# Entry of a Strassen MLP: eight channel pairs instead of four start on the first token half, the second half's sums move from POOL to DVE, and the squared ReLU moves from DVE to ACT

## The chip, the cores and the metric

The kernel runs on one core of one Trainium2 chip. The metric is the device time of one execution in microseconds (us). Engines: PE is TensorE, DVE is VectorE, ACT is ScalarE, POOL is GpSimd, SP is the engine whose queue issues most of the DMA transfers.

## The reference, cut to what matters

The program is a whole two-block network (a gated recurrent mixer with a mixture of experts, then attention with an MLP). The change lies in its last part, the MLP of the second block: 1024 tokens, 1024 features, 4096 hidden channels, a squared ReLU, all in float32.

```python
h = rms_norm_2(x, norm_mlp[i]) * (1 + sc_f) + sh_f
x = x + g_f * (jnp.square(jax.nn.relu(h @ w_mlp_in[i])) @ w_mlp_out[i])
```

## The kernel before, in words

**Split numbers.** Each float32 operand of a matmul is split into a high and a low part: `Net.split` (L65 to L67) lets ACT write the high part (L66) and DVE the difference (L67). A product of two 128-row tiles is three matmuls (L854 to L856).

**Seven products.** `h @ w_mlp_in` is done by Strassen's scheme in Winograd's form. The tokens are two halves of 512, the features two halves of 512, and the hidden channels 16 *pairs* of 2 x 128. For each pair n there are seven products, numbered by o; one *step* is one product of one pair, 12 matmuls of 128x512 into one PSUM tile (`X`, or `Z` for o = 3). The whole is 112 steps. The moving operands are the seven tiles `hc[0]` to `hc[6]`. `hc[0]` and `hc[1]` are the first token half as it is; `hc[2]` to `hc[6]` are sums in which the second half takes part. So products 0 and 1 of a pair need only the first half, and the other five need the second half. The weights (`wc`) of products 0, 1, 4 and 6 are raw blocks; those of 3, 2 and 5 are sums that POOL makes in `Mlp.prep` (L1648 to L1656).

**Order.** `Mlp.order` lists the steps: first products 0 and 1 of pairs 0 to 3 (steps 0 to 7), then product 3 of pairs 0 and 1 (steps 8 and 9), products 2, 4, 5, 6 of the same, and so on two pairs at a time. PE keeps this order. `Mlp.todo` lists the weight loads in the same order; a pair that is begun early has its first block loaded twice. The raw blocks pass through a ring of six tiles (`wr`), in which the eight normed token tiles also stand at first. `prep` runs three steps ahead (`LOOK`), with four `wc` buffers.

**The second half.** Ahead of steps 2 to 5, `half1(kk)` (L2350 to L2370) turns one quarter of the features of the second half: 8 transposes on PE into PSUM (`hTp`, two buffers), two evacuations on ACT (L2357), then the sums: two subtractions on DVE (L2360, L2361) make `T`, three on POOL (L2363, L2364, L2368) and one on DVE (L2369) make the others, and five splits write `hc[3]`, `hc[5]`, `hc[2]`, `hc[4]`, `hc[6]`. `T` and POOL's weight sum S1 share the two buffers `hTt`. The temporaries lie in `x2a`, whose tokens were written to DRAM before (`x2d`) and are loaded back later.

**After a product.** For o = 0 ACT copies PSUM to a tile `s`; for the others DVE adds to it. A finished sum passes `Mlp.inner` (L1707): one DVE instruction does max(s,0)*s, and SP stores the result (L1708) to DRAM. After step 111, `Mlp.block` multiplies by `w_mlp_out`; its operands come back through the same ring and are split into the places of `hc` (`item`).

DVE, ACT, POOL and SP keep the order that the scheduler gave them; an instruction that waits holds up all that stand behind it on its engine.

Of the kernel before, what the change touches and what calls it, by code (L numbers as in the profile page):

```python
# [19 lines left out]
P = 128  # L20
# [1555 lines left out]
class Mlp:  # L1576
# [54 lines left out]
    def prep(self, g):  # L1631
# [4 lines left out]
        first = n < 4 and o < 2  # L1636
# [23 lines left out]
        wc = self.wc[g] = self.early.pop(0) if self.early else self.wp.tile([P, 2, 4, P], F32R, name="wc", bufs=4)  # L1660
# [9 lines left out]
    def step(self, g):  # L1670
# [3 lines left out]
        self.prep(g + self.LOOK)  # L1674
# [7 lines left out]
        if o == 0:  # L1682
            s = self.s[n] = self.wp.tile([P, 512], F32, name="s", bufs=4)
            nc.scalar.activation(s, pt, AF.Copy)
        elif o == 1:
            s = self.wp.tile([P, 512], F32, name="c", bufs=4)
            v.tensor_add(s, self.s[n], pt)
            self.inner(s, n, 0, 0)
        elif o == 2:
            v.tensor_add(self.s[n], self.s[n], pt)  # L1690
        elif o == 4:
            s = self.s[n]
            u = self.u[n] = self.wp.tile([P, 512], F32, name="c", bufs=4)
            r = self.wp.tile([P, 512], F32, name="c", bufs=4)
            v.tensor_add(u, s, pt)
            z = self.Z.pop(n)
            v.tensor_add(r, u, z)
            v.tensor_add(s, s, z)
            self.inner(r, n, 1, 1)
        elif o > 4:  # L1700
            s = (self.s if o == 5 else self.u).pop(n)
            v.tensor_add(s, s, pt)
            self.inner(s, n, *((0, 1) if o == 5 else (1, 0)))

    def inner(self, s, n, i, m):

        self.net.nc.vector.scalar_tensor_tensor(s, s, 0.0, s, op0=ALU.max, op1=ALU.mult)  # L1707
        self.net.nc.sync.dma_start(self.rD[n][i][:, HALF[m]], s)  # L1708


    def open_second(self, x2, gate_row, out):
        self.x2, self.out = x2, out
        self.gb = self.wp.tile([P, D], F32, name="mgb", tag="wc", bufs=4)
# [18 lines left out]
    def block(self, c):  # L1732
        net = self.net
        nc, v = net.nc, net.nc.vector
        for tt in range(TT):
# [9 lines left out]
            for n in range(2):  # L1745
                cc = HALF[n]
                t = self.wp.tile([P, 512], F32, name="s", bufs=4)
                v.tensor_mul(t, pts[n], self.gb[:, cc])  # L1748
                v.tensor_add(self.x2[tt][:, cc], self.x2[tt][:, cc], t)
# [21 lines left out]
def program(net, ctx, I, out, dbg):  # L1771
# [21 lines left out]
    x2d = scratch("x2d", [512, D])  # L1793
# [460 lines left out]
    with ExitStack() as cx:  # L2254
# [9 lines left out]
        def units(tts):  # L2264
            for tt, n in tts:
# [6 lines left out]
                    if n == 1 and tt < 4:  # L2272
# [39 lines left out]
        x2 += [xb.tile([P, D], F32, name=f"x2_{tt}") for tt in range(4, 8)]  # L2312
# [7 lines left out]
        mlp.early = []  # L2320

# [28 lines left out]
        def half1(kk):  # L2350

            t12, t22 = tmp[:, kk, :], tmp[:, 4 + kk, :]
            for k, t in ((kk, t12), (kk + 4, t22)):
                pt = nps.tile([P, 512], F32, name="hTp", bufs=2)
                for i, xn in enumerate(xns):
                    nc.tensor.transpose(pt[:, i * P:(i + 1) * P], xn[:, k * P:(k + 1) * P], net.ident)
                nc.scalar.activation(t, pt, AF.Identity, scale=sc3[:, k:k + 1], bias=sh3[:, k:k + 1])  # L2357
            T = np_.tile([P, 512], F32, name="hTt", bufs=2)
            h = [hc[o][:, kk] for o in range(7)]
            v.tensor_sub(T, t12, h[0][:, 0, :].bitcast(F32))  # L2360
            v.tensor_sub(T, T, h[0][:, 1, :].bitcast(F32))  # L2361
            net.split(h[3][:, 0, :], h[3][:, 1, :], T)
            nc.gpsimd.tensor_sub(t12, t22, t12)  # L2363
            nc.gpsimd.tensor_sub(T, t22, T)  # L2364
            net.split(h[5][:, 0, :], h[5][:, 1, :], t22)
            net.split(h[2][:, 0, :], h[2][:, 1, :], T)
            net.split(h[4][:, 0, :], h[4][:, 1, :], t12)
            nc.gpsimd.tensor_sub(t22, h[1][:, 0, :].bitcast(F32), T)  # L2368
            v.tensor_add(t22, t22, h[1][:, 1, :].bitcast(F32))  # L2369
            net.split(h[6][:, 0, :], h[6][:, 1, :], t22)  # L2370

        with tc.manual_schedule(engines={mybir.EngineType.PE}):
            for g in range(len(mlp.order)):
                if g in range(2, 6):
                    half1(g - 2)
# [7 lines left out]
                if g == 20:  # L2383
# [4 lines left out]
                if g >= len(mlp.order) - 6:  # L2388
                    mlp.item()
            for _ in range(2):  # L2390
# [23 lines left out]
```

## Time and profile before

| | |
|---|---|
| median of 3 runs | 2606.24 us (2605.98 to 2619.54) |
| the profiled execution | 2609.64 us, of which the span of the profile is 2607.9 us |
| PE busy | 2386.0 us, 91% of the span |
| DVE, ACT, POOL busy | 77%, 52%, 21% of the span |
| the MLP's steps | from 1911.7 us to 2250.8 us of the span |
| the MLP's second matmul | from 2250.8 us to the end |

Times inside the span count from its start. Busy shares are means over stages with different limits. For a change in one stage what counts is what PE waits for in that stage, since PE is fully busy from 1971 us to the end.

### The profile page before, as it was taken

What the parts mean: (1) busy time and instruction counts of PE and PEld (TensorE: products, weight loads), DVE (VectorE), ACT (ScalarE), POOL (GpSimd) and SP (SyncE); (2) the same over time, 40 slices, a digit from 0 to 9 for tenths busy, and PEclk for the clock granted to TensorE, in tenths of its full rate; (3) what the DMA queues carried; (4) which work ended last, traced back from release to release, by engine and by line L of the source; (5) the groups of instructions that cost most, each with busy time, mean ns of one, the idle gap of its engine ahead of it and who ended that gap; (6) DMA issues with size and microseconds to landing.
All of it is one profiled execution on the core that took longest, in us unless ns stands there. A gap on an engine that the chain in (4) does not pass through costs nothing. (4 is left out here: it accounts for less than half of the span.)

```text
span 2607.9 us, 34881 instructions
## 1 busy us (share of the span) xinstructions
PE 2386.0 (91%) x11789; PEld 1920.5 (74%) x11789; DVE 2014.5 (77%) x3648; ACT 1346.6 (52%) x2447; POOL 551.4 (21%) x527
## 2 busy tenths in 40 slices
PE   6899989959999999985899999997979999999999
PEld 5576767747776766543898999986757888888887
DVE  6888886877989788996787777877668667776664
ACT  5555563236868677775677777775332222321210
POOL 1202121042224243532000000013335233000000
PEclk9899999969999999997999999998989999999999
DMA  7445565769999999994022122017334333532211
GB/s 263 135 138 164 177 203 165 258 231 304 366 340 377 329 362 320 365 366 143 18 50 50 50 49 50 23 39 204 138 89 129 97 113 121 186 103 91 98 65 65
DMA packets 258866, 445.64 MB, mean 171 GB/s; under 512 B 22096, under 2 KB 101828, under 8 KB 258684
## 3 DMA queue, kind: packets, MB, share of 16 engines
q1 hardware_dynamic: 250532, 424.45, 48.8%
q0 software_dynamic: 8032, 18.89, 3.2%
q8 instruction: 94, 1.54, 0.3%
q14 instruction: 88, 0.72, 0.1%
q10 hardware_dynamic: 120, 0.03, 0.0%
HBM read 395.62 MB, written 54.73 MB: 173 GB/s over the span
## 5 line engine op out<-in xcount | busy, mean ns | idle before, releaser
L67 DVE TENSOR_TENSOR wl<-wr,wh 128x1024 fp32r<-128x1024 f32 x210 | 249.9, 1230 | 28.3 <-ACT wh L66 25.7
L66 ACT ACTIVATE wh<-wr 128x1024 fp32r<-128x1024 f32 x216 | 220.6, 1054 | 87.4 <-PE po L464 30.6
L67 DVE TENSOR_TENSOR wl<-x,wh 128x1024 fp32r<-128x1024 f32 x164 | 192.6, 1219 | 26.8 <-ACT wh L66 25.4
L591 POOL DMA_INDIRECT x1d<-y,gidx x56 | 156.5, 2795 | 235.1 <-DMA x1d<-y,gidx 107.3
L66 ACT ACTIVATE hc<-wr 128x1024 fp32r<-128x1024 f32 x64 | 64.6, 1056 | 266.8 <-PE X L855 244.8
L856 PE MATMUL X<-hc 128*128 128x512 f32 x512 | 200.3, 391 | 0.0
L854 PE MATMUL X<-hc 128*128 128x512 f32 x512 | 200.3, 391 | 0.0
L855 PE MATMUL X<-hc 128*128 128x512 f32 x512 | 199.7, 390 | 0.0
L66 ACT ACTIVATE wh<-x 128x1024 fp32r<-128x1024 f32 x168 | 172.8, 1058 | 43.0 <-issue 9.1
L854 PE MATMUL pj<-xh,h2h 128*128 128x384 f32 (+1 forms) x512 | 190.2, 372 | 0.8 <-DVE V L1433 0.7
L1748 DVE TENSOR_TENSOR s<-X,mgb 128x512 f32<-128x512 f32 x128 | 86.5, 690 | 123.2 <-PE X L856 123.1
L855 PE MATMUL pj<-xh,h2l 128*128 128x384 f32 (+1 forms) x512 | 175.9, 344 | 0.0
L856 PE MATMUL pj<-xl,h2h 128*128 128x384 f32 (+1 forms) x512 | 174.6, 342 | 0.0
L854 PE MATMUL X<-hc,wc 128*128 128x512 f32 x384 | 151.9, 396 | 3.4 <-ACT rs_y L91 3.4
L855 PE MATMUL X<-hc,wc 128*128 128x512 f32 x384 | 151.7, 395 | 0.2 <-DVE wc L67 0.2
L856 PE MATMUL X<-hc,wc 128*128 128x512 f32 x384 | 151.4, 394 | 0.0
L782 DVE SCALAR_TENSOR_TENSOR aacc<-aw,cs,aacc 128x512 f32<-128x512 f32 x160 | 128.2, 803 | 25.0 <-DMA aw<-in_w_ada 12.5
L66 ACT ACTIVATE wc<-wr 128x512 fp32r<-128x512 f32 x96 | 60.5, 633 | 166.6 <-PE X L856 118.7
L1501 ACT ACTIVATE Sx<-Sx,mx 128x128 f32<-128x128 f32 (+7 forms) x128 | 99.0, 773 | 41.0 <-DVE mx L1496 40.5
L67 DVE TENSOR_TENSOR pl<-pT,ph 128x512 fp32r<-128x512 f32 (+1 forms) x160 | 100.8, 634 | 23.0 <-ACT ph L66 19.6
L855 PEld LDWEIGHTS X<-hc 128*128 128x128 f32 x512 | 96.1, 188 | 21.2
L856 PEld LDWEIGHTS X<-hc 128*128 128x128 f32 x512 | 96.1, 188 | 21.1
(562 smaller groups left out, 6871.0 us busy)
## 6 DMA issues: line engine op xcount, KB each, us to landing
wr<-in_w_expert_down SPq DMA_DIRECT2D x43, 1024.0 KB
wr<-in_w_expert_up SPq DMA_DIRECT2D x33, 1024.0 KB
x<-in_w_expert_gate SPq DMA_DIRECT2D x32, 1024.0 KB
wr<-in_w_expert_gate SPq DMA_DIRECT2D x32, 1024.0 KB
x<-in_w_expert_up SPq DMA_DIRECT2D x31, 1024.0 KB
aw<-in_w_ada SPq DMA_DIRECT2D x48, 512.0 KB
x<-in_w_expert_down SPq DMA_DIRECT2D x21, 1024.0 KB
aw<-in_ada_w SPq DMA_DIRECT2D x40, 512.0 KB
```

Source lines behind the costliest of these rows:

```text
L66: self.nc.scalar.activation(hi, src, AF.Copy)
L67: (v or self.nc.vector).tensor_sub(lo, src, hi.bitcast(F32))
L591: nc.gpsimd.indirect_dma_start(out=m.xd, out_offset=bass.IndirectOffsetOnAxis(ap=gi[0:r], axis=0), in_=y[o:o + r], in_offset=None, bounds_ ...
L782: nc.vector.scalar_tensor_tensor(acc, t[:, r, :], ccol[:, q:q + 1], acc, op0=ALU.mult, op1=ALU.add)
L854: nc.tensor.matmul(pt, sh, mh, start=first, stop=False)
L855: nc.tensor.matmul(pt, sl, mh, start=False, stop=False)
L856: nc.tensor.matmul(pt, sh, ml, start=False, stop=last)
L1501: nc.scalar.activation(Sx[:, 0:wd], Sx[:, 0:wd], AF.Exp, bias=mx[:, m - 1:m], scale=-1.0, accum_out=sm[:, q:q + 1])
L1748: v.tensor_mul(t, pts[n], self.gb[:, cc])
```

## The change

1. Products 0 and 1 of eight pairs come first, not of four: steps 0 to 15, so that the first step that needs the second half is step 16, not step 8. Four more blocks of 512 KB are loaded. `LOOK` is 4, with five `wc` buffers; at step 4 nothing is prepared and at step 5 two steps' weights.
2. `half1` is cut up. `turn(k)` keeps the transposes and the evacuation ahead of steps 2 to 5. The sums and splits are a generator of 12 parts, one after each step from step 2 to step 13. All six sums are on DVE, none on POOL.
3. `inner` is two ACT instructions (Relu, Square) in place of one on DVE.
4. The sums `s` of products 0 stand in the tile of the other four token tiles (`x2b`), which are therefore written to `x2d` as well and loaded back after the steps.

```diff
-    LOOK = 3
+    LOOK = 4
+    EARLY = 8
...
-        self.order = [(0, 0), (0, 1), (1, 0), (1, 1), (2, 0), (2, 1), (3, 0), (3, 1)]
-        self.todo = [("p", n) for n in range(4)]
+        self.order = [(n, o) for n in range(self.EARLY) for o in range(2)]
+        self.todo = [("p", n) for n in range(self.EARLY)]
...
-            self.order += duo(a, (3, 2, 4, 5, 6) if a < 4 else (0, 1, 3, 2, 4, 5, 6))
+            self.order += duo(a, (3, 2, 4, 5, 6) if a < self.EARLY else (0, 1, 3, 2, 4, 5, 6))
...
-        self.prep(g + self.LOOK)
+        for i in (8, 9) if g == 5 else () if g == 4 else (g + self.LOOK,):
+            self.prep(i)
...
-            s = self.s[n] = self.wp.tile([P, 512], F32, name="s", bufs=4)
+            s = self.s[n] = self.sums[:, n % 8, :]
...
-        self.net.nc.vector.scalar_tensor_tensor(s, s, 0.0, s, op0=ALU.max, op1=ALU.mult)
+        self.net.nc.scalar.activation(s, s, AF.Relu)
+        self.net.nc.scalar.activation(s, s, AF.Square)
         self.net.nc.sync.dma_start(self.rD[n][i][:, HALF[m]], s)
...
-                    if n == 1 and tt < 4:
+                    if n == 1:
                         nc.sync.dma_start(x2d[tt * P:(tt + 1) * P, :], x2[tt])
...
-            nc.gpsimd.tensor_sub(t12, t22, t12)
-            nc.gpsimd.tensor_sub(T, t22, T)
...
-            nc.gpsimd.tensor_sub(t22, h[1][:, 0, :].bitcast(F32), T)
-            v.tensor_add(t22, t22, h[1][:, 1, :].bitcast(F32))
...
+        def half1():
+
+            for kk in range(4):
+                t12, t22 = tmp[:, kk, :], tmp[:, 4 + kk, :]
+                T = np_.tile([P, 512], F32, name="hTt", bufs=2)
+                h = [hc[o][:, kk] for o in range(7)]
+                v.tensor_sub(T, t12, h[0][:, 0, :].bitcast(F32))
+                v.tensor_sub(T, T, h[0][:, 1, :].bitcast(F32))
+                net.split(h[3][:, 0, :], h[3][:, 1, :], T)
+                yield
+                v.tensor_sub(T, t22, T)
+                net.split(h[2][:, 0, :], h[2][:, 1, :], T)
+                v.tensor_sub(t12, t22, t12)
+                net.split(h[4][:, 0, :], h[4][:, 1, :], t12)
+                yield
+                net.split(h[5][:, 0, :], h[5][:, 1, :], t22)
+                v.tensor_sub(T, h[1][:, 0, :].bitcast(F32), T)
+                v.tensor_add(T, T, h[1][:, 1, :].bitcast(F32))
+                net.split(h[6][:, 0, :], h[6][:, 1, :], T)
+                yield
...
                 mlp.step(g)
-                if g == 20:
+                if g > 1:
+                    next(parts, None)
+                if g == 40:
```

Three places show how the built programs differ. The first is POOL from its first instruction in the MLP. Before, with the four quarters' sums (`x2a`, `hTt_20194` to `hTt_20337`) and the weight sums of pair 0 (`wr_20354`, `wr_20358`) in one queue:

```order
L2363 TENSOR_TENSOR x2a_18854<-x2a_18854 128x512
L1648 TENSOR_TENSOR hTt_20370<-wr_20354 128x512
L1650 TENSOR_TENSOR wr_20354<-wr_20358,wr_20354 128x512
L1651 TENSOR_TENSOR wr_20358<-hTt_20370,wr_20358 128x512
L1656 TENSOR_TENSOR wr_20358<-wr_20358 128x512
L2364 TENSOR_TENSOR hTt_20337<-x2a_18854,hTt_20337 128x512
L2368 TENSOR_TENSOR x2a_18854<-hc1_19613,hTt_20337 128x512
```

Now only the weight sums of pairs 0 and 1 stand there:

```order
L1649 TENSOR_TENSOR hTt_20504<-wr_20311 128x512
L1651 TENSOR_TENSOR wr_20311<-wr_20325,wr_20311 128x512
L1652 TENSOR_TENSOR wr_20325<-hTt_20504,wr_20325 128x512
L1657 TENSOR_TENSOR wr_20325<-wr_20325 128x512
L1649 TENSOR_TENSOR hTt_20529<-wr_20313 128x512
```

The last quarter's two sums no longer stand behind pair 0's weights; twelve POOL instructions are gone, and nothing in the MLP's entry waits for POOL but the weights of products 3, 2 and 5.

The second place is ACT around the last two pairs of transposes before (`hTp_20278`, `hTp_20284` are the third quarter's):

```order
L2357 ACTIVATE x2a_18854<-hTp_20235,cols2_4810,sc3_4815 128x512
L66 ACTIVATE hc2_20132<-hTt_20194 128x512
L66 ACTIVATE hc5_20135<-x2a_18854 128x512
L66 ACTIVATE hc3_20133<-hTt_20241 128x512
L66 ACTIVATE hc4_20134<-x2a_18854 128x512
L66 ACTIVATE hc6_20136<-x2a_18854 128x512
L66 ACTIVATE wc_20258<-wr_20145 128x512
L2357 ACTIVATE x2a_18854<-hTp_20278,cols2_4810,sc3_4815 128x512
```

and now, from the second to the third quarter (`hTp_20226`, `hTp_20259`):

```order
L2360 ACTIVATE x2a_18854<-hTp_20226,cols2_4810,sc3_4815 128x512
L66 ACTIVATE wc_20232<-wr_20133 128x512
L66 ACTIVATE hc2_20138<-hTt_20215 128x512
L66 ACTIVATE hc4_20140<-x2a_18854 128x512
L66 ACTIVATE wc_20319<-wr_20303 128x512
L2360 ACTIVATE x2a_18854<-hTp_20259,cols2_4810,sc3_4815 128x512
L1709 ACTIVATE c_20248<-c_20248 128x512
L2360 ACTIVATE x2a_18854<-hTp_20265,cols2_4810,sc3_4815 128x512
L1710 ACTIVATE c_20248<-c_20248 128x512
```

Between two evacuations there stood five splits of the sums; now there stand two, and Relu and Square (L1709, L1710) between others.

The third place is DVE ahead of the weights of step 17, the second step that needs the second half (`wc_20531`, made from POOL's sum `hTt_20529`); `hTt_20499` is the last quarter's `T`:

```order
L67 TENSOR_TENSOR wc_20506<-hTt_20504,wc_20506 128x512
L2372 TENSOR_TENSOR hTt_20499<-x2a_18854,hTt_20499 128x512
L2374 TENSOR_TENSOR x2a_18854<-x2a_18854 128x512
L67 TENSOR_TENSOR hc5_20141<-x2a_18854,hc5_20141 128x512
L67 TENSOR_TENSOR hc2_20138<-hTt_20499,hc2_20138 128x512
L67 TENSOR_TENSOR hc4_20140<-x2a_18854,hc4_20140 128x512
L67 TENSOR_TENSOR wc_20531<-hTt_20529,wc_20531 128x512
L1689 TENSOR_TENSOR c_20547<-x2b_19608,X_20534 128x512
```

Before, these stood ahead of the weights of the same product (`wc_20394`):

```order
L67 TENSOR_TENSOR hc3_20133<-hTt_20337,hc3_20133 128x512
L67 TENSOR_TENSOR wc_20372<-hTt_20370,wc_20372 128x512
L1687 TENSOR_TENSOR c_20388<-s_20323,X_20375 128x512
L67 TENSOR_TENSOR hc2_20132<-hTt_20337,hc2_20132 128x512
L2369 TENSOR_TENSOR x2a_18854<-x2a_18854,hc1_19613 128x512
L1707 SCALAR_TENSOR_TENSOR c_20388<-c_20388 128x512
L67 TENSOR_TENSOR wc_20394<-hTt_20392,wc_20394 128x512
```

The last operand `hc3` that both steps read is now done before pair 0's weights, with five of the last quarter's operations between the two weights. The loads of ACT's tables are three in either program.

## Rows read from the trace of the kernel before

**Rows 1.** Windows: stretch, length, busy (count) PE, PEld, DVE, ACT, POOL; clock; DMA.

```profile
1911.00:1930.20 19.20, 18.31 (x84) 14.84 (x84) 14.51 (x22) 10.76 (x21) 5.77 (x4) 0.91 0.34 96
1930.20:1971.00 40.80, 22.76 (x70) 16.67 (x69) 36.56 (x38) 16.01 (x28) 26.93 (x17) 0.71 0.44 126
2040.00:2240.00 200.00, 200.00 (x877) 164.21 (x876) 140.68 (x195) 59.01 (x91) 64.50 (x40) 1.00 0.40 126
2240.00:2602.00 362.00, 362.00 (x1584) 296.84 (x1582) 233.41 (x325) 56.16 (x58) 0.00 (x0) 1.00 0.28 95
```

**Rows 2.** Waits of PE, 1905 to 2608 us: total us, times, longest.

```profile
PE Z L854 <- ACT wc L66: 7.3, 1, 7.3
PE Z L855 <- DVE wc L67: 6.8, 2, 4.1
PE hTp L2356 <- ACT x2a L2357: 4.0, 2, 3.3
```

**Rows 3.** Timeline of PE: start, duration, and what ended the idle time before.

```profile
1911.69 0.47 PE L854 MATMUL X<-hc,wc 128*128 128x512 f32 x1 [3.38 <-ACT rs_y L91]
...
1919.37 1.03 PE L2356 MATMUL hTp<-ident,wr 128*128 128x128 f32 x8
1920.16 0.48 PE L854 MATMUL X<-hc,wc 128*128 128x512 f32 x1
...
1959.33 0.63 PE L856 MATMUL Z<-hc,wc 128*128 128x512 f32 x1
...
1963.60 0.54 PE L854 MATMUL Z<-hc,wc 128*128 128x512 f32 x1
1966.84 0.56 PE L855 MATMUL Z<-hc,wc 128*128 128x512 f32 x1 [2.70 <-DVE wc L67]
```

**Rows 4.** Chain that ended last, in order of time: start, duration, what.

```profile
1956.55 1.59 POOL wr L1656
1958.14 1.70 POOL hTt L2364
...
1965.04 1.76 DVE wc L67
```

**Rows 5.** Groups of instructions, 1911 to 1971 us: count, busy us, mean ns, idle before.

```profile
L2357 ACT ACTIVATE x2a<-hTp,cols,sc 128x512 f32<-128x512 f32 x8 | 5.8, 771 | 0.0
L2356 PE MATMUL hTp<-ident,wr 128*128 128x128 f32 x32 | 5.3, 313 | 4.0 <-ACT x2a L2357 4.0
```

**Rows 6.** Timeline of DVE, POOL and SP's queue at four places.

```profile
1917.93 0.69 DVE L67 TENSOR_TENSOR wc<-wr,wc 128x512 fp32r<-128x512 f32 x1 [2.61 <-ACT wc L66]
...
1944.95 0.69 DVE L67 TENSOR_TENSOR hc<-hTt,hc 128x512 fp32r<-128x512 f32 x1
1945.55 0.69 DVE L2360 TENSOR_TENSOR hTt<-x2a,hc 128x512 f32<-128x512 f32 x1
1945.71 1.65 POOL L2364 TENSOR_TENSOR hTt<-x2a,hTt 128x512 f32<-128x512 f32 x1 [2.07 <-DVE hc L67]
1946.15 1.76 DVE L67 TENSOR_TENSOR hc<-x2a,hc 128x512 fp32r<-128x512 f32 x1
...
1975.44 0.38 SPq L1620 DMA_DIRECT2D wr<-in_w_mlp_in  x1
1979.70 1.29 POOL L1648 TENSOR_TENSOR hTt<-wr 128x512 f32<-128x512 f32 x1 [11.78 <-DMA wr<-in_w_mlp_in]
```

**Rows 7.** Groups of instructions, 1975 to 2240 us.

```profile
L66 ACT ACTIVATE wc<-wr 128x512 fp32r<-128x512 f32 x81 | 51.5, 635 | 157.3 <-PE X L856 114.9 <-PE Z L856 26.0 <-issue 10.1
L1707 DVE SCALAR_TENSOR_TENSOR c<-c 128x512 f32<-128x512 f32 x40 | 27.2, 681 | 0.0
L66 ACT ACTIVATE hc<-wr 128x1024 fp32r<-128x1024 f32 x9 | 9.5, 1060 | 7.0 <-DMA wr<-rD 3.9 <-DMA wr<-in_w_mlp_out 2.4 <-PE X L856 0.7
```

**Rows 8.** Groups of instructions, 1850 to 1971 us: Square with a sum.

```profile
L820 ACT ACTIVATE wr<-x 128x1024 f32<-128x1024 f32 x4 | 4.2, 1060 | 23.1 <-DVE x L2270 23.1
```

**Rows 9.** Timeline of PE: the first matmul of `Mlp.block`.

```profile
2250.80 0.39 PE L854 MATMUL X<-hc 128*128 128x512 f32 x1
```

More of the change, by code (lines that the diff above doesn't have):

```diff
@@ L1635, in prep @@
         gp = self.net.nc.gpsimd
-        first = n < 4 and o < 2
+        first = n < self.EARLY and o < 2
         f = self.raw["p" if first else "f", n]
@@ L1659, in prep @@
             src = A22
[L1660 removed]
+        wc = self.wc[g] = self.early.pop(0) if self.early else self.wp.tile([P, 2, 4, P], F32R, name="wc", bufs=5)
         self.net.split(wc[:, 0], wc[:, 1], src)
@@ L1692, in step @@
             s = self.s[n]
-            u = self.u[n] = self.wp.tile([P, 512], F32, name="c", bufs=4)
-            r = self.wp.tile([P, 512], F32, name="c", bufs=4)
+            u = self.u[n] = self.wp.tile([P, 512], F32, name="c", bufs=5)
+            r = self.wp.tile([P, 512], F32, name="c", bufs=5)
             v.tensor_add(u, s, pt)
@@ L1712, in open_second @@
         self.x2, self.out = x2, out
-        self.gb = self.wp.tile([P, D], F32, name="mgb", tag="wc", bufs=4)
+        self.gb = self.wp.tile([P, D], F32, name="mgb", tag="wc", bufs=5)
         self.net.nc.sync.dma_start(self.gb, gate_row.to_broadcast([P, D]))
@@ L1746, in block @@
                 cc = HALF[n]
-                t = self.wp.tile([P, 512], F32, name="s", bufs=4)
+                t = self.wp.tile([P, 512], F32, name="c", bufs=5)
                 v.tensor_mul(t, pts[n], self.gb[:, cc])
@@ L1792, in program @@
     x1d = scratch("x1d", [S, D])
-    x2d = scratch("x2d", [512, D])
+    x2d = scratch("x2d", [S, D])
     rD = [[scratch(f"rD{n}_{i}", [P, S]) for i in range(2)] for n in range(Mlp.NP)]
@@ L2311, in program @@
         xb = net.pool(cx, "x2b")
-        x2 += [xb.tile([P, D], F32, name=f"x2_{tt}") for tt in range(4, 8)]
+        x2b = xb.tile([P, 4, D], F32, name="x2b")
+        x2 += [x2b[:, tt, :] for tt in range(4)]
         hc = {o: xb.tile([P, 4, 2, 512], F32R, name=f"hc{o}") for o in range(2)}
@@ L2320, in program @@
         mlp.early = []
+        mlp.sums = x2b.rearrange("p t (a n) -> p (t a) n", a=2)
         def norm(tt, t):
@@ L2348, in program @@
         tmp = x2a.rearrange("p t (a n) -> p (t a) n", a=2)
[L2350 to L2362, printed above, removed]
-            nc.gpsimd.tensor_sub(t12, t22, t12)
-            nc.gpsimd.tensor_sub(T, t22, T)
-            net.split(h[5][:, 0, :], h[5][:, 1, :], t22)
-            net.split(h[2][:, 0, :], h[2][:, 1, :], T)
-            net.split(h[4][:, 0, :], h[4][:, 1, :], t12)
-            nc.gpsimd.tensor_sub(t22, h[1][:, 0, :].bitcast(F32), T)
-            v.tensor_add(t22, t22, h[1][:, 1, :].bitcast(F32))
-            net.split(h[6][:, 0, :], h[6][:, 1, :], t22)
@@ new lines, in turn @@
+        def turn(k):
+            pt = nps.tile([P, 512], F32, name="hTp", bufs=2)
+            for i, xn in enumerate(xns):
+                nc.tensor.transpose(pt[:, i * P:(i + 1) * P], xn[:, k * P:(k + 1) * P], net.ident)
+            nc.scalar.activation(tmp[:, k, :], pt, AF.Identity, scale=sc3[:, k:k + 1], bias=sh3[:, k:k + 1])
+        def half1():
[17 more added lines that the diff above has]
+                yield
@@ L2372, in program @@
+        parts = half1()
         with tc.manual_schedule(engines={mybir.EngineType.PE}):
@@ L2374, in program @@
                 if g in range(2, 6):
-                    half1(g - 2)
+                    for k in (g - 2, g + 2):
+                        turn(k)
                     if g == 5:
@@ L2389, in program @@
                     mlp.item()
+            for tt in range(4, 8):
+                nc.sync.dma_start(x2[tt], x2d[tt * P:(tt + 1) * P, :])
             for _ in range(2):
```

2 lines of the change are left out of this document (1 added, 1 removed).

## The prediction

> **What bounds the kernel now.** I read the windows by stage first. From 2040 to 2240 us and from 2240 us to the end PE is busy throughout at full clock, so nothing there but fewer matmuls could make the end come sooner; 877 matmuls in 200.00 us are 0.228 us each, and a step of 12 is 2.74 us [rows 1]. The stretch before is another thing: from 1930.20 to 1971.00 us PE is busy 22.76 of 40.80 us, with a mean granted clock of 0.71 [rows 1]. Whatever PE loses there the end pays in full, because PE is never idle behind it.
>
> The list of PE's waits says for what: 7.3 us until ACT had the high part of the first weights of product 3, 6.8 us until DVE had low parts of such weights (two waits), 4.0 us until ACT had emptied a PSUM buffer of the transposes [rows 2]. PE's timeline shows that the waits drag a second loss behind them. Behind the second of them, ten matmuls from 1959.33 to 1963.60 us are 0.43 us apart: that is the lower of the two clock levels, 1.2 GHz and not 2.4, and it lasts for some us after PE is at work again [rows 3].
>
> The chain that ended last shows who was late. It goes through POOL: a weight sum (L1656), then the last quarter's second sum (L2364), and from there over ACT and DVE to the low part at 1965.04 us [rows 4]. POOL's sums are also slow, and slow for DVE: beside a POOL sum of 1.65 us, a DVE subtraction with both inputs in SBUF took 1.76 us; the two ahead of it took 0.69 us and began 0.60 us apart [rows 6].
>
> **How much there is to win.** In the 40.80 us stand 70 instructions: eight transposes (the last of the four groups that make the 32 [rows 5]) and 62 matmuls. At full rate these are 62 x 0.228 = 14.1 us and 1.0 us (a group of eight took 1.03 us [rows 3]), together 15.1 us. So 40.80 - 15.1 = 25.7 us are lost: 18.1 us of waits and 7.6 us of low clock and overlap. In the stretch ahead of it 84 instructions (60 matmuls, 24 transposes) should take 13.7 + 2.4 us, and take 18.5 us from the first matmul at 1911.69 us on [rows 3]; these 2.4 us, low clock after the idle time ahead of the MLP, I leave in place, since the change does nothing ahead of step 0.
>
> **Part by part.**
>
> *Steps 8 to 15 moved ahead.* No matmul is added. Step 16 is the first to need the second half. With PE at full rate it comes 14 steps (2 to 15) and four groups of transposes after 1919.37 us; a group takes 0.79 us of PE's time, from 1919.37 to 1920.16 us [rows 3]. That is 1919.4 + 38.4 + 3.2 = 1961.0 us, and step 17 follows at 1963.7 us. Before, the same product of the same pair had its last late weights at 1966.8 us [rows 3]. So if the work on the second half were done no sooner than before, PE would still wait 3 us; what it has lost is the chain through POOL, and what it has gained is DVE work. Whether that is done by 1964 us is worked out below.
>
> *Transposes.* Before, five splits of late sums stood on ACT between two evacuations; now two do, and Relu and Square come in between. None of them waits for POOL. An evacuation takes 0.77 us [rows 5]; PE comes for the buffer a step of 2.74 us later. I cost these waits at 0 (before 4.0 us, plus their low clock). If an evacuation came behind four other ACT instructions of 0.63 us and a wait for DVE, PE would wait a us or so; that is within the range.
>
> *Sums to DVE.* From the low part at 1917.93 us [rows 6] to that of step 17's weights DVE has 61 instructions, as the program lists them. At 0.60 us apart that is 36.6 us, until 1954.5 us. POOL now runs eight weight sums of about 1.65 us shortly before step 16, 13 us of contention. In the third place above, six DVE instructions with both inputs in SBUF stand in that time, each 1.76 - 0.69 = 1.07 us longer: 6.4 us, so 1960.9 us. What is not in this sum is how long DVE waits for ACT's high parts. In the stretch before it was busy 36.56 of 40.80 us [rows 1]; waits of 10% here too, some 4 us, would bring 1965 us against a need at 1964 us. The wait of PE at step 17 thus lies between 0 (no waits, 1961 us) and 7 us (eight slowed instructions in POOL's 13 us and not six, 2 us, and twice the waits, 8 us: 1971 us). I take 1 us, the sum with the share of waits that the rows show.
>
> *Squares to ACT.* No row shows a Relu by itself; I price both by the copy of 128x512, 0.63 us, and by Square on twice the width, 1.06 us [rows 7, 8], so 1.26 us on ACT in place of 0.68 us on DVE. Up to the weights of step 17 ACT has 60 instructions from about 1917 us on, just ahead of DVE's low part at 1917.93 us: 8 x 0.77 + 52 x 0.63 = 38.9 us even without overlap, so 1956 us, earlier than DVE. In the steady steps ACT's idle time ahead of its weight splits alone is 157.3 us of 265 us [rows 7]; of the 64 squares 56 fall behind step 15, and 56 x 1.26 = 71 us fit into it. I cost them at 0; the cover is ACT's idle time and the four steps by which `prep` runs ahead. The Trainium skill speaks against this edit: the page "ScalarE: Activation LUTs", section "Rules for kernel authors", wants relu and mul on VectorE, not on ScalarE. By the rows, the rule is right on busy time (1.26 us against 0.68 us), and the sum is the same with it or without, as long as neither engine is the one that PE waits for; what it would do if ACT were that engine is rival D.
>
> *Loads and stores.* Four more blocks of weights, four more token tiles out and back: 12 transfers of 512 KB on SP's queue. A weight load landed 4.3 us after its issue (1975.44 to 1979.70 us [rows 6]). Step 8, the first with a block of the new four, is due at 1919.4 + 3.2 + 6 x 2.74 = 1939.0 us, and the ring's last slots come free with step 5's transposes at about 1931 us. Of these 8 us a load and its split (4.3 + 0.63 + 0.69 us) leave 2 us, so they are covered. The reloads go into buffers that become free pair by pair. The DMA engines were busy 40% of the time in the steps [rows 1]. Cost 0; what it costs without cover is rival C.
>
> **The sum.** -25.7 us for the stretch, +1 us at step 17, 0 for the rest: -24.7 us. The profiled execution took 2609.64 us, which gives 2585. It was 3.4 us above the median of the runs, so against the median of 2606.24 us I forecast 2582 us.
>
> **Rivals.** Measurement of this kernel can tell about 0.5%, 13 us, from no change.
>
> *A, the forecast* (0.60): 2582 us, own range 2578 to 2587.
>
> *B, DVE becomes the bound of the entry* (0.27). PE waits 5 us at step 17, between my value and the upper end, then runs some ten matmuls at 0.43 us, 2 us more, and waits once more about 2 us at step 18 or 19, whose weights stand behind on DVE. 2606.2 - 25.7 + 9 = 2589.5 us. For it: 61 instructions and 13 us of contention in 44 us leave no slack in my sum. Against it: the sum ends on the needed time, not 5 us behind.
>
> *C, the win is given back at the start of `block`* (0.08). Its operands come through SP's queue behind the stores, which now wait for Square on ACT, and their splits (1.06 us) stand on ACT between Relu and Square. Before, nine of them were done by 2240 us [rows 7] and `block` began at 2250.80 us [rows 9]: 10.8 us of cover. If each of the eight that the first block needs came 3 us later, PE would wait 24 - 11 = 13 us: 2606.2 - 24.7 + 13 = 2595 us, and with low clock and a second wait 2600 us. It decides from 1.4 us a split on. Against it: `prep` and loads run further ahead than before.
>
> *D, slower: ACT is too slow in the steady steps* (0.05). A Relu waits for a DVE sum, and the weight splits behind it on ACT wait too. If PE then lost 0.7 us in each of the 96 steps from 16 on, 67 us, the time would be 2606.2 - 24.7 + 67 = 2649 us; it is slower than before from 0.26 us a step. Against it: ACT's 157.3 us of idle time [rows 7]. The rule of the Trainium skill's page "ScalarE: Activation LUTs" would speak for it.
>
> That the change does not do what it says is excluded by the listing of the built program: POOL's twelve sums are gone and 16 steps stand ahead of the first `Z`.
>
> **Range and chances.** 2576 takes in the forecast with the 2.4 us of low clock gone as well; 2594 takes in B with some us more. Outside lie C, D and tails, about 0.17. Faster by over 0.5%: A, B and half of C, 0.90; same 0.06; slower 0.04.
>
> **What the profile will show.** Right, if PE's waits from 1911 us on come to 1 to 2 us instead of 18.1 us, the first `Z` starts at about 1961 us, the clock stays 1.00 from 1916 us on, `block` begins at about 2226 us, and POOL's first instruction in the entry is a weight sum. B would show as a wait of `Z` L855 for DVE's `wc` with DVE fully busy ahead of it and instructions of 1.7 us in it. C shows as waits of `X` for `hc` at 2226 us, D as many short waits of `X` for ACT's `wc`. Wrong altogether, if PE has as many matmuls at 0.43 us as before.

## The result, and the profile after

| | before | after |
|---|---|---|
| median of the runs | 2606.63 us (4 runs, 2605.98 to 2619.54) | 2581.76 us (4 runs, 2577.85 to 2583.37) |
| ratio after to before | | 0.9892, 95% interval 0.9865 to 0.9920 |
| profiled execution, its span | 2609.64, 2607.9 us | 2582.41, 2580.4 us |
| first matmul of step 0 | 1911.69 us | 1910.34 us |
| first matmul of `block` [rows 9] | 2250.80 us | 2223.21 us |
| the 112 steps between these two | 339.11 us | 312.87 us |
| from the first matmul of `block` to the end of the span | 357.1 us | 357.2 us |

Faster by 24.9 us, about 1.1%. The change lies in the 112 steps, and so does the gain: they became 26.2 us shorter. The stretch behind them is as long as before. The 1.35 us ahead of step 0 belong to a part that the change hardly touches; it varies from execution to execution by much more (last section). So from here on each kernel is judged by its runs and by **the length of the 112 steps in its profile**, which leaves that part out. Medians and ratios leave out one execution that lies far off all others (2740.64 us, of the kernel with the squares back on DVE).

Windows of after, in the columns of [rows 1]:

```profile
1911.00:1930.20 19.20, 19.18 (x93) 15.90 (x94) 15.89 (x29) 14.63 (x27) 0.00 (x0) 0.91 0.48 137
1930.20:1971.00 40.80, 40.80 (x178) 33.09 (x177) 37.15 (x50) 26.65 (x48) 12.83 (x8) 1.00 0.63 189
2012.41:2212.41 200.00, 200.00 (x878) 164.54 (x877) 118.06 (x154) 108.12 (x170) 56.03 (x40) 1.00 0.43 139
2040.00:2240.00 200.00, 200.00 (x877) 164.34 (x876) 119.06 (x157) 105.61 (x165) 44.27 (x32) 1.00 0.48 157
```

The second row is the whole result. In the same 40.80 us in which PE did 70 instructions before, it now does 178, at full clock. The third row shows the price of the steady steps; it is the 200 us that lie as far ahead of `block` as the window from 2040 to 2240 us did before. ACT went from 59.01 to 108.12 us of work, DVE from 140.68 to 118.06, the DMA share from 0.40 to 0.43, and PE's count is the same to one, 878 matmuls. (In the last row, the old window, 17 us belong to `block`; PE's count is 877 there.)

All waits of PE from 1890 us to the end, where [rows 2] had 18.1 us in three kinds:

```profile
PE X L854 <- ACT rs_y L91: 3.4, 1, 3.4
PE X L855 <- DVE wc L67: 0.2, 1, 0.2
```

Both stand ahead of and in step 0; the first was there before ([rows 3], at 1911.69 us). Behind step 0 PE never waits. Its timeline at four places: step 0, the first group of transposes, steps 16 and 17 (the first products 3), and the first matmul of `block`:

```profile
1910.34 0.47 PE L854 MATMUL X<-hc,wc 128*128 128x512 f32 x1 [3.38 <-ACT rs_y L91]
...
1918.03 1.04 PE L2359 MATMUL hTp<-ident,wr 128*128 128x128 f32 x8
...
1960.69 0.40 PE L854 MATMUL Z<-hc,wc 128*128 128x512 f32 x1
...
1963.41 0.39 PE L854 MATMUL Z<-hc,wc 128*128 128x512 f32 x1
1963.64 0.39 PE L855 MATMUL Z<-hc,wc 128*128 128x512 f32 x1
...
2223.21 0.39 PE L854 MATMUL X<-hc 128*128 128x512 f32 x1
```

The matmul at 1963.64 us is the first to read the low part of step 17's weights. DVE ahead of it, and POOL:

```profile
1949.86 0.68 DVE L1689 TENSOR_TENSOR c<-x2b,X 128x512 f32<-128x512 f32 x1
1951.79 1.23 DVE L67 TENSOR_TENSOR wc<-hTt,wc 128x512 fp32r<-128x512 f32 x1 [1.26 <-ACT wc L66]
1952.95 1.79 DVE L2372 TENSOR_TENSOR hTt<-x2a,hTt 128x512 f32<-128x512 f32 x1
...
1961.49 1.77 DVE L67 TENSOR_TENSOR wc<-hTt,wc 128x512 fp32r<-128x512 f32 x1
...
1949.41 1.68 POOL L1649 TENSOR_TENSOR hTt<-wr 128x512 f32<-128x512 f32 x1 [77.71 <-DVE hc L67]
...
1959.38 1.63 POOL L1652 TENSOR_TENSOR wr<-hTt,wr 128x512 f32<-128x512 f32 x1
1961.10 1.62 POOL L1657 TENSOR_TENSOR wr<-wr 128x512 f32<-128x512 f32 x1
```

Step 17's low part is written by 1961.49 + 1.77 = 1963.26 us: 0.4 us ahead of the matmul that reads it. The entry is no longer late, but it is not comfortable either. POOL does nothing in the entry but eight weight sums, and they fall on the last six DVE operations in SBUF ahead of step 17, which stand 1.70 us apart instead of 0.60 (the one at 1951.79 us, ahead of them, is slowed in part), as the one in [rows 6] was slow beside a quarter's sum.

Groups of ACT: the first three rows from 1911 to 1971 us, the last three from 1975 to 2212 us (columns as in [rows 5, 7]):

```profile
L2360 ACT ACTIVATE x2a<-hTp,cols,sc 128x512 f32<-128x512 f32 x8 | 5.9, 772 | 0.0
L1710 ACT ACTIVATE c<-c 128x512 f32<-128x512 f32 x8 | 5.0, 629 | 0.2
L1709 ACT ACTIVATE c<-c 128x512 f32<-128x512 f32 x8 | 5.0, 626 | 6.6 <-DVE c L1689 6.6
...
L66 ACT ACTIVATE wc<-wr 128x512 fp32r<-128x512 f32 x72 | 45.4, 631 | 72.1 <-PE X L856 55.8 <-PE Z L856 16.3
L1709 ACT ACTIVATE c<-c 128x512 f32<-128x512 f32 x36 | 22.8, 633 | 15.8 <-DVE c L1699 12.0 <-DMA wr<-in_w_mlp_in 2.4
L1710 ACT ACTIVATE c<-c 128x512 f32<-128x512 f32 x36 | 22.8, 632 | 1.1
```

Relu and Square take 0.63 us each. ACT still stands idle for 72.1 us ahead of its weight splits, and what it waits for there is PE.

### The profile page after: what moved, and what is told of

Same layout as the page of the kernel before. It is cut to its first block, busy times and chain, and to the rows that moved or that the text cites. A ratio compares the mean times of both kernels' runs of the same rounds, so it can differ in the third digit from the quotient of the medians.

```text
span 2580.4 us, 34978 instructions
## 1 busy us (share of the span) xinstructions
PE 2373.7 (92%) x11789; PEld 1913.3 (74%) x11789; DVE 1971.6 (76%) x3596; ACT 1419.8 (55%) x2575; POOL 522.1 (20%) x515
## 4 chain that ended last, share of the span: by engine, by line
PE 71%; DVE 14%; ACT 5%; DMA 5%; issue 4%; POOL 1%; SPq 0%; DVEq 0%; ACTq 0%; POOLq 0%
PE X L856 8%; PE X L854 8%; PE X L855 8%; PE pj L854 4%; PE pj L855 4%; PE pj L856 3%; DVE wl L67 2%; PE po L1513 2%; PE op L856 2%; PE op L855 2%; PE op L854 2%; PE pT L1524 2%; DVE aacc L782 2%; PE pt L534 1%; PE po L577 1%
## 5 line engine op out<-in xcount | busy, mean ns | idle before, releaser
L67 DVE TENSOR_TENSOR wl<-x,wh 128x1024 fp32r<-128x1024 f32 x164 | 192.6, 1219 | 26.8 <-ACT wh L66 26.2
L1751 DVE TENSOR_TENSOR c<-X,mgb 128x512 f32<-128x512 f32 x128 | 86.7, 689 | 129.1 <-PE X L856 126.0
L855 PEld LDWEIGHTS X<-hc 128*128 128x128 f32 x512 | 96.1, 188 | 21.2
L856 PEld LDWEIGHTS X<-hc 128*128 128x128 f32 x512 | 96.1, 188 | 21.2
L854 PEld LDWEIGHTS X<-hc 128*128 128x128 f32 x512 | 96.1, 188 | 20.5
```

What stands on the lines that cost most here:

```text
L67: (v or self.nc.vector).tensor_sub(lo, src, hi.bitcast(F32))
L854: nc.tensor.matmul(pt, sh, mh, start=first, stop=False)
L855: nc.tensor.matmul(pt, sl, mh, start=False, stop=False)
L856: nc.tensor.matmul(pt, sh, ml, start=False, stop=last)
```

## The experiments

**My theory**: PE came to the first products 3 before the second half's sums were done. Eight pairs give it work meanwhile; moving sums and squares only decides whether DVE is done in time. **The rivals**: POOL's sums in the chain were the cause, and the eight pairs do little; or the eight pairs are the whole cause, and the two moves do nothing; or the squares on ACT cost something.

The three parts of the change can be made one by one. All eight combinations, and six pairs as a ninth kernel (ratios against before, from runs on the same chip; the steps from the profile; waits of PE behind the one ahead of step 0):

| pairs first | sums | squares | median, ratio with interval | 112 steps | PE waits |
|---|---|---|---|---|---|
| 4 | POOL | DVE | before | 339.11 us | 18.3 us |
| 4 | POOL | ACT | 2606.60, 0.9988 [0.9978, 0.9999] | 338.55 us | 16.9 us |
| 4 | DVE | DVE | 2602.00, 0.9980 [0.9970, 0.9991] | 333.26 us | 12.3 us |
| 4 | DVE | ACT | 2601.43, 0.9974 [0.9957, 0.9990] | 331.31 us | 14.8 us |
| 8 | POOL | DVE | 2590.71, 0.9946 [0.9930, 0.9962] | 320.72 us | 5.2 us |
| 8 | POOL | ACT | 2587.69, 0.9938 [0.9918, 0.9958] | 317.38 us | 3.8 us |
| 8 | DVE | DVE | 2586.06, 0.9918 [0.9904, 0.9933] | 317.39 us | 2.4 us |
| 8 | DVE | ACT | after | 312.87 us | 0.2 us |
| 6 | DVE | ACT | 2589.41, 0.9919 [0.9903, 0.9934] | 319.77 us | 4.3 us |

All rows have 0.2 us of these waits inside step 0. By the runs alone the last four rows can hardly be told apart, since their intervals overlap that of after (0.9865 to 0.9920). They differ in the steps, read from one profile each; two profiles of after differ there by 0.6 us.

The rows with 8 and with 6 hold more than the pairs: `LOOK` 4, the fifth `wc` buffer and the cut-up `half1` come with them. No kernel here has these with four pairs, so what they give by themselves is not shown. That the pairs count is: with the same three, six pairs take 6.9 us more than eight.

**Eight pairs alone** (with `LOOK` and the cut-up `half1` of after; sums on POOL, squares on DVE):

```diff
-                v.tensor_sub(T, t22, T)
+                nc.gpsimd.tensor_sub(T, t22, T)
...
-                v.tensor_sub(t12, t22, t12)
+                nc.gpsimd.tensor_sub(t12, t22, t12)
...
-                v.tensor_sub(T, h[1][:, 0, :].bitcast(F32), T)
+                nc.gpsimd.tensor_sub(T, h[1][:, 0, :].bitcast(F32), T)
...
-        self.net.nc.scalar.activation(s, s, AF.Relu)
-        self.net.nc.scalar.activation(s, s, AF.Square)
+        self.net.nc.vector.scalar_tensor_tensor(s, s, 0.0, s, op0=ALU.max, op1=ALU.mult)
```

> Eight pairs first, but sums on POOL and squares on DVE as before: the first part of the change alone. Theory: the 14 steps of PE work from step 2 to step 16 cover most of a chain that before ended 7 to 12 us late; what stays is one or two waits at the first products 3, 4 to 6 us in all with low clock behind: 2588 to 2593 us, so about two thirds of the 25 us. Rival 1 (POOL's sums are the whole cause): 2598 us or more. Rival 2 (cover is the whole cause): 2582 to 2584 us.

Measured: 2590.71 us, the steps 18.4 us shorter than before. This one part is 70% of the 26.2 us. Its waits of PE:

```profile
PE X L855 <- DVE wc L67: 2.7, 3, 2.1
PE Z L855 <- DVE wc L67: 2.5, 2, 2.0
```

Both rivals fall here. With POOL's sums left in place most of the gain is there, and yet not all of it: 5.2 us of waits remain, all for DVE.

**Sums moved to DVE alone**, in the kernel before:

```diff
-            nc.gpsimd.tensor_sub(t12, t22, t12)
-            nc.gpsimd.tensor_sub(T, t22, T)
+            v.tensor_sub(t12, t22, t12)
+            v.tensor_sub(T, t22, T)
...
-            nc.gpsimd.tensor_sub(t22, h[1][:, 0, :].bitcast(F32), T)
+            v.tensor_sub(t22, h[1][:, 0, :].bitcast(F32), T)
```

> The kernel before with one part of the change: the three sums of each quarter that were on POOL go to DVE; four pairs first, squares on DVE. DVE gets 12 operations of 0.60 us more, 7 us, and loses the contention of 12 POOL sums, some 12 x 1.07 us = 13 us; the chain through POOL is gone. Theory (cover first): with four pairs PE still comes to step 8 long before the sums are done, so waits of 10 to 14 us stay of 18.1: 2596 to 2603 us. Rival (POOL's sums are the whole cause): 2590 us or less.

Measured: 2602.00 us, the steps 5.9 us shorter. POOL has left the chain, and its place is taken by DVE. PE's waits:

```profile
PE Z L855 <- DVE wc L67: 6.4, 2, 5.9
PE X L855 <- DVE wc L67: 4.4, 2, 4.2
...
PE Z L854 <- ACT wc L66: 1.5, 1, 1.5
```

The chain that ended last [rows 4] named POOL, truly; taking POOL out of it gave a fifth of the gain, because the next engine was nearly as late. A chain says who was last, not by how much.

**Squares moved to ACT alone**, in the kernel before (the two lines of `inner` from the change):

> The kernel before with the square alone moved to Relu and Square on ACT. Ahead of the first products 3 that takes about three operations of 0.68 us off DVE, 2 us, and puts six of 0.63 us on ACT between the evacuations. Theory: nothing that can be measured, 2602 to 2607 us. Rival (DVE alone is the bound of the entry): 2595 us or less. Rival 2 (ACT too slow in the steady steps): 2610 us or more.

Measured: 2606.60 us, ratio 0.9988, the steps 0.6 us shorter: as good as nothing, as expected. PE still waits 12.5 us at `Z`.

**Both moves, four pairs**:

> The kernel before with sums on DVE and squares on ACT, and still only four pairs first: the change without its eight pairs. Theory: DVE is relieved by both, but 61 operations less some 12 for four pairs, about 30 us of DVE work, still stand against six steps and four groups of transposes, 20 us of PE work, from step 2 to step 8; waits of about 8 to 12 us stay, with low clock: 2594 to 2601 us. Rival (eight pairs are not needed once POOL and the squares are out of the way): 2587 us or less.

Measured: 2601.43 us, the steps 7.8 us shorter: 0.4 us above the expected span, and with 14.8 us more waits than the 8 to 12 us in it. PE's waits at the first products 3:

```profile
PE Z L855 <- DVE wc L67: 8.5, 1, 8.5
PE Z L854 <- ACT wc L66: 4.4, 1, 4.4
```

With four pairs no division of the sums among the engines tried here is fast enough.

**Eight pairs, sums on POOL again** (squares stay on ACT):

> The kernel after, with three of the six sums of each quarter back on POOL; eight pairs and squares on ACT stay. Twelve POOL sums of 1.65 us are 20 us of contention; at 1.07 us for each DVE operation in SBUF beside one, some 12 of them cost DVE 13 us and the 12 sums taken away give 7 us back, so DVE is 6 us later against 3.1 us of slack. Theory (cover first, POOL second): a wait of 2 to 4 us for DVE at the first products 3 and some at the transposes, with low clock 2586 to 2591 us. Rival 1 (POOL's sums are the whole cause, the eight pairs do little): 2597 us or more. Rival 2 (the eight pairs are the whole cause): as after, within 2 us of it.

Measured: 2587.69 us, the steps 4.5 us longer than after, in the expected span. The waits for DVE, 3.1 us behind step 0, have the size that I had said, but the longer one is not at a product 3:

```profile
1960.44 0.50 PE L855 MATMUL X<-hc,wc 128*128 128x512 f32 x1 [2.12 <-DVE wc L67]
...
1967.20 0.50 PE L855 MATMUL Z<-hc,wc 128*128 128x512 f32 x1 [0.94 <-DVE wc L67]
```

The first is in step 15, a product 1 whose weights stand behind the sums on DVE, the second in step 17; 0.6 us more are at the transposes. The low clock that I had expected did not come: behind both the matmuls are 0.23 us apart. The rest of the 4.5 us is what a wait costs beyond its idle time, some 0.3 us each here, until the matmuls follow one another as closely as before.

**Eight pairs, squares on DVE again**:

> The kernel after, with the square back in one DVE instruction; all else as after. In the trace of after DVE ends the low part of step 17's weights at 1963.26 us and PE comes to them at 1966.36 us: 3.1 us of slack. Six squares now stand ahead of it on DVE, 6 x 0.60 to 0.68 us = 3.6 to 4.1 us. Theory (eight pairs give the cover, squares on ACT only keep DVE just below it): PE waits 0.5 to 1.5 us for DVE at the first products 3, with or without a us or two of low clock: 2583 to 2586 us. Rival 1 (squares on ACT carry the win): 2592 us or more. Rival 2 (squares on ACT cost something in the steady steps): 2580 us or less.

This expectation has a wrong reading in it: PE comes to the low part of step 17 at 1963.64 us, as shown above, and not at 1966.36 us, which is step 18. The slack is 0.4 us and not 3.1 us, and six more operations of 0.60 us should then cost some 3 us of wait. Measured: 2586.06 us, at the upper end of the expected span, the steps 4.5 us longer than after. The wait is in step 18, not in step 17: the scheduler put two splits of the last quarter behind step 17's weights, so that these are done only 0.6 us later than in after, and step 18's weights come behind the two splits and a square. PE at the second matmul of step 18:

```profile
1966.50 0.39 PE L854 MATMUL X<-hc,wc 128*128 128x512 f32 x1
1969.08 0.64 PE L855 MATMUL X<-hc,wc 128*128 128x512 f32 x1 [2.19 <-DVE wc L67]
1969.52 0.63 PE L856 MATMUL X<-hc,wc 128*128 128x512 f32 x1
1969.94 0.63 PE L854 MATMUL X<-hc,wc 128*128 128x512 f32 x1
```

The reader sees both halves of the price: 2.19 us of wait, and then eight matmuls 0.43 us apart (three of them shown), at the lower clock. Rival 2 falls too: with the squares on DVE nothing became faster anywhere.

**Six pairs first**: `EARLY = 6`, with the 12 parts of `half1` dealt out over steps 2 to 9:

```diff
-    EARLY = 8
+    EARLY = 6
...
-                if g > 1:
-                    next(parts, None)
+                for _ in range((0, 0, 1, 1, 2, 2, 2, 2, 1, 1)[g] if g < 10 else 0):
+                    next(parts, None)
```

> The kernel after with six pairs first, not eight: the first product 3 is step 12, 4 steps or 10.9 us sooner; the parts of the second half's sums stand closer together. PE would then want the low part at 1966.4 - 10.9 = 1955.5 us; two pairs have three DVE operations each ahead of it, some 4 us less of DVE work, so it is done at 1963.3 - 4 = 1959.3 us. Theory (cover against DVE's work): PE waits about 4 us in all, with low clock behind it 2586 to 2590 us. Rival (six pairs are cover enough, for there is slack all along): 2582 us. Rival 2 (each pair less costs the whole 5.5 us of its steps): 2593 us or more.

Measured: 2589.41 us, the steps 6.9 us longer than after. The waits came to 4.3 us, as expected in sum, though the slack in the text is the same wrong one. More of them are for ACT than for DVE:

```profile
PE Z L854 <- ACT wc L66: 2.6, 2, 1.9
PE Z L855 <- DVE wc L67: 1.5, 2, 0.7
```

Two pairs less take 10.9 us of cover away, but also their own work on DVE and ACT; that is how I read it that the price is 6.9 us and not 10.9.

**All weight sums of pairs 0 and 1 on DVE**, to see whether POOL really is what makes DVE slow:

```diff
-        gp = self.net.nc.gpsimd
+        gp = self.net.nc.vector if n < 2 else self.net.nc.gpsimd
```

> The kernel after with the eight weight sums of pairs 0 and 1 on DVE too, so that POOL is idle until step 20 or so. In the trace of after six DVE operations with both inputs in SBUF, beside those sums, took 1.78 us and stood 1.70 us apart. If POOL's sums make them slow: every DVE operation takes 0.69 us again, 8 x 0.60 = 4.8 us are added and 6 x 1.10 = 6.6 us saved, and the low part of step 17 is done about 2 us sooner than in after (there 53 us after the first matmul of step 0). Rival (DVE is slow there for a reason of its own, such as the buffers that it reads): the same operations stay at 1.7 us and it is done 5 us later, with a wait at step 17. Time as after within the spread of single runs, or up to 5 us more by the rival.

Measured: the steps 312.89 us, no wait behind step 0 (one run, 2588.08 us, with the lower clock ahead of the MLP that the last section describes). DVE at the places of the slow operations:

```profile
1956.89 0.69 DVE L2372 TENSOR_TENSOR hTt<-x2a,hTt 128x512 f32<-128x512 f32 x1
1957.49 0.69 DVE L2374 TENSOR_TENSOR x2a<-x2a 128x512 f32<-128x512 f32 x1
...
1966.07 0.69 DVE L67 TENSOR_TENSOR wc<-hTt,wc 128x512 fp32r<-128x512 f32 x1
```

The same operations take 0.69 us, not 1.78. Step 17's low part is done 1966.76 - 1916.16 = 50.6 us after the first matmul of step 0, against 1963.26 - 1910.34 = 52.9 us in after: 2.3 us sooner although nine operations more stand ahead of it on DVE (five of the eight weight sums, and four that stood behind it in after). The rival falls: POOL's sums were what made these operations slow.

**The weights of steps 0 and 1 split earlier.** What is left in after is the idle time ahead of step 0. This kernel makes these splits ahead of the norm of token tile 6, into the place of two token tiles that are already stored (`x2a` becomes four tiles for that, of which two are given out twice):

```diff
+            if tt == 6:
+                mlp.early = [xa.tile([P, 2, 4, P], F32R, name="wc", tag=f"xa{t}", bufs=1) for t in (1, 3)]
+                for g in range(2):
+                    mlp.prep(g)
             xns[tt - 4] = norm(tt, xns[tt - 4])
...
-        for g in range(Mlp.LOOK):
+        for g in range(2, Mlp.LOOK):
```

> The kernel after, with the weights of steps 0 and 1 split ahead of the norms of the last two token tiles, into the place of two token tiles that are already stored. In the trace of after PE is idle for 3.38 us ahead of step 0 until these splits, which stand on ACT behind a Square of 1.06 us, and for 0.21 us more until the low part, and has 3 us of low clock behind it. Theory: what is left is the 0.7 us until DVE has read the last PSUM tile of the output projection, and the low clock behind the idle time is gone: 2576 to 2578 us. Rival: the norm of the last tile or the PSUM buffers then hold step 0 up for as long: 2581 to 2583 us.

Measured: 2576.39 us (4 runs), ratio 0.9887 [0.9873, 0.9901]. Its timeline of PE, from the last matmul of the output projection:

```profile
1903.46 0.39 PE L856 MATMUL op<-owl,oyh 128*128 128x512 f32 x1
1904.63 0.50 PE L854 MATMUL X<-hc,wc 128*128 128x512 f32 x1 [0.78 <-DVE opt L1276]
1904.97 0.40 PE L855 MATMUL X<-hc,wc 128*128 128x512 f32 x1
...
1954.67 1.77 DVE L67 TENSOR_TENSOR wc<-hTt,wc 128x512 fp32r<-128x512 f32 x1
1956.50 0.50 PE L855 MATMUL Z<-hc,wc 128*128 128x512 f32 x1
```

The wait is 0.78 us, not 3.38, and the next matmuls are at full clock. The last two rows are the low part of step 17 and the matmul that reads it: the slack of after is used up, and this matmul comes 0.45 us behind the first of its step instead of 0.23. To be sure of the size I ran it once more beside the kernel after:

> The kernel with the weights of steps 0 and 1 split ahead of the last norms once more, beside the kernel after. Theory: 4 to 6 us less than after, of which 3 us are the idle time ahead of step 0 and 1 to 3 us the low clock behind it; from the last matmul of the output projection to the first of block 313 us against 316.6 us. Rival (the first result came from a stretch ahead of the MLP that happened to be short): both the same within 2 us, and the difference of that stretch too.

> The kernel after once more, beside the next one, for a comparison in the same rounds: 2580 to 2584 us. The part of the program that differs, from the first matmul of step 0 to the first of block, should again take 312 to 313 us (after: 2223.21 - 1910.34 = 312.87 us), and the step 17 low part should be done 2 to 4 us before PE wants it.

Measured in those rounds: after 2581.18 us, 0.9897 [0.9876, 0.9917] (steps 313.47 us, no wait behind step 0); the earlier splits 2583.50 us, 0.9895 [0.9874, 0.9916]. By the runs that is no gain, against 2576.39 us the first time. From the last matmul of the output projection to the first of `block`, which takes in all that this edit changes, it is one: 312.75 and 312.77 us in its two profiles, 316.64 and 317.24 us in those of after. So the edit is worth 4 us where it stands, shown twice; that it makes the whole program faster than after is not shown, since the runs of either spread over 10 us and more. Between its two profiles 8.25 us lie ahead of the MLP (the last matmul of the output projection is at 1911.71 us in the second), so the rival is right about the 5 us between the first medians in so far as the stretch ahead decides it as much as the edit. The expectation of the kernel after repeats the wrong slack of step 17; in this second profile it is again 0.4 us (done at 1962.83 us, read at 1963.20 us).

## Why the prediction was right

**What bounds the kernel, and how much there is to win.** The forecast of 2582 us, against 2581.76, came from one stretch: 25.7 us lost from 1930.20 to 1971.00 us. The steps became 26.2 us shorter; half a us of that I can't assign. That forecast and median meet to 0.3 us is luck: the runs of after spread over 5.5 us, and the forecast has a wait of 1 us in it that did not come.

**Steps 8 to 15 moved ahead.** Step 16 was forecast for 1961.0 us and began at 1960.69; step 17 for 1963.7, and began at 1963.41, all without a wait. The mechanism holds; the closeness of the times is in part luck, because this execution began step 0 1.35 us sooner than the one before. Counted from the first matmul of step 0, step 16 came after 50.35 us and not after 49.3. The matmuls of steps 6 to 15 were 0.233 us apart, those from step 16 on 0.227, where I had taken the 0.228 of the steady steps for both; with the transposes this makes PE 1.0 us later than forecast. The sentence that with the work done no sooner PE would still wait 3 us was too mild: eight pairs alone left 5.2 us of waits, and with low clock behind them the steps were 7.9 us longer than after.

**Transposes.** No wait, as costed.

**Sums to DVE.** Six operations beside POOL's sums were forecast at 1.07 us more each, 6.4 us. There were six, 1.70 us apart instead of 0.60, 6.6 us. The wait of 1 us at step 17 was not there: the low part was done 0.4 us before PE read it. It is the one term of the sum that failed. To see why, both ends have to be counted from the same place. From the low part with which my count began (1917.93 us before, 1916.60 us now) to the end of step 17's low part I had forecast 47.1 us, and the same 61 instructions took 46.7 us. The total is right, its parts are not: DVE's waits, which I took at 4 us, were 1.8 us of idle time, the longest 1.26 us ahead of 1951.79; but nearly 2 us that I had not costed took their place, in the seventh operation that a POOL sum slowed in part (the next one began 1.16 us behind it) and in gaps a little over 0.60 us. The larger share of the difference is on PE's side, the 1.0 us above: had PE come as early as forecast, it would have waited about 0.6 us, by an estimate from these times. So the wait of 1 us became none by two small errors that lay the same way, not by reasoning, and rival B, for which it was the door, fell by 0.4 us of slack. That this was close the experiments show: sums back on POOL or squares back on DVE, each alone, cost 4.5 us, the first by 3.7 us of waits at full clock, the second by 2.2 us of wait and eight matmuls at the lower clock.

**Squares to ACT.** 1.26 us a pair of instructions was forecast and measured. It cost nothing in the steady steps: PE has no wait there, and 878 matmuls in 200 us where before it had 877. The rule of the Trainium skill's page "ScalarE: Activation LUTs" (section "Rules for kernel authors"; relu and mul to VectorE) would have kept the square on DVE. The trace agrees with it on busy time (1.26 against 0.68 us) and not on the result: in the entry DVE is the engine that PE nearly waits for, and the move is worth 4.5 us there. That is the case of another page of the Trainium skill, "Perfetto Trace Analysis" (section "Optimizing Scalar/DVE Operations"), by which work may go to ScalarE where DVE is saturated. The trace agrees: DVE was busy 37.15 of 40.80 us in the entry, and by the steps the move gave 0.6 us in the kernel before (as much as two profiles of one kernel differ by), 2.0 with the sums on DVE, 3.3 with eight pairs, and 4.5 with both.

**Loads and stores.** No wait for a load or a store appears on PE behind step 0. C is out: `block` began at 2223.21 us without a wait. D is out: PE has no wait for ACT's `wc`. `block` was forecast for about 2226 us; of the 3 us 1.35 us are the earlier step 0, 1 us is the wait that did not come, and half a us is the one that I can't assign.

**What the prediction did not see** is how the gain divides. It spoke of the chain through POOL first. By the steps, the eight pairs alone (with `LOOK` and the cut-up `half1`) bring 18.4 us, the sums alone 5.9, the squares alone 0.6; together these are 24.9 of 26.2 us. That the sum nearly closes does not mean that the parts are independent: with eight pairs in place the squares bring 3.3 us instead of 0.6, and the sums 3.3 instead of 5.9; the one rise and the other fall nearly cancel.

## What to carry to other kernels

Where PE waits at a point at which a second batch of operands becomes due, look first for work that needs only the first batch and can be put ahead of that point; spreading the preparation over other engines came second here (7.8 of 26.2 us), since it met the next engine that was nearly as late. Ask of an engine that comes out of the chain who would be last without it.

Where DVE's operations have both inputs in SBUF, ask what GpSimd's elementwise work costs DVE: 13 us of POOL sums cost it 6.6 us here, more than the eight sums would have cost on DVE itself (8 x 0.60 = 4.8 us).

Measure a change of 1% by the length of its own stretch in the profile too: two profiles of a kernel agreed there to 0.6 us where its runs spread over 10.

## What the runs showed of the hardware that was not expected

**The clock in a stage that no kernel here changes.** In four of the 13 profiled executions (the second run of the earlier splits, six pairs, squares alone, and the weight sums on DVE) the mean granted clock was 0.97 from 1400 to 1720 us, in the attention stage ahead of the MLP, in the other nine 1.00 (0.99 in one). Windows of after, and of the second run of the earlier splits:

```profile
1400.00:1440.00 40.00, 37.96 (x253) 35.18 (x253) 31.41 (x99) 29.51 (x79) 3.39 (x14) 1.00 0.24 64
1400.00:1720.00 320.00, 310.33 (x2058) 288.52 (x2058) 256.27 (x794) 233.41 (x605) 30.43 (x118) 1.00 0.18 47
```

```profile
1400.00:1440.00 40.00, 37.95 (x242) 35.08 (x241) 30.74 (x94) 29.33 (x76) 3.75 (x16) 0.96 0.25 64
1400.00:1720.00 320.00, 310.31 (x2003) 288.25 (x2002) 249.94 (x769) 228.76 (x592) 30.02 (x116) 0.97 0.17 46
```

PE is as busy in both, to 0.02 us, and does 55 matmuls less in the second: the time is lost at the lower clock, not in waits. The waits are the same: in either execution PE stands idle five times in this stage until ACT is done, 1.66 to 1.99 us each. Here is the second of them, first in after, then in the second run of the earlier splits, with the clock and two matmuls behind it:

```profile
1480.91 0.55 PE L1524 MATMUL pT<-ident,Sx 128*128 128x128 f32 x3 [1.66 <-ACT sr L1567]
```

```profile
1479.08 0.55 PE L1524 MATMUL pT<-ident,Sx 128*128 128x128 f32 x3 [1.66 <-ACT sr L1567]
1480.00:1485.00 5.00, 5.00 (x25) 4.76 (x24) 2.68 (x8) 2.54 (x6) 0.82 (x4) 0.66 0.59 169
1481.68 0.52 PE L854 MATMUL pj<-xh,h2h 128*128 128x384 f32 x1
1482.00 0.52 PE L855 MATMUL pj<-xh,h2l 128*128 128x384 f32 x1
```

These matmuls are 0.32 us apart, at the lower of the two levels; elsewhere in the stage they are 0.18 us apart. In the four executions the clock falls like this within some us of each of the five waits, in the eight at 1.00 behind none of them, in the one at 0.99 behind the last alone. Each time costs some 1.7 us, together 8 us and more. At the last matmul of the output projection the second run of the earlier splits was at 1911.71 us, the first at 1903.46 us. It is not all that varies ahead of the MLP: this matmul lies at 1899.92 to 1907.92 us in the nine others, and at 1911.71 to 1916.20 us in the four. Of the runs without a profile only the mean clock is known, and it does not sort them well: the four of after have their longest but one at the highest clock, 0.972. What decides on which side an execution falls is not shown; a median of five runs can differ by some us through it.

**The size of the contention between POOL and DVE.** The page "GPSIMD Engine Reference" of the Trainium skill (section "Key points") says that GpSimd shares its SBUF interfaces with VectorE and contends with its instructions that have two SBUF inputs. The trace agrees and gives the size: 1.77 to 1.79 us for 128x512 in float32 beside a POOL sum, 0.69 us without, while the one addition with an operand in PSUM that ran beside such a sum (L1689, at 1949.86 us) took 0.68 us. The two engines keep step: the POOL sums of 1959.38 and 1961.10 us also begin 1.72 us apart, one for each DVE operation.
